# Order of the matmuls within an expert's weight block, and selections of results placed in groups of four

## The chip, the cores and the metric

The kernel runs on one core of one Trainium2 chip. The metric is the device time of one execution in microseconds (us). Engines are named as in the profile: PE is TensorE (PEld its weight loads), DVE is VectorE, ACT is ScalarE, POOL is GpSimd, SP is SyncE, whose queue issues the weight transfers.

## What is computed

Two layers over 256 context and 512 latent tokens of width 1024. Each has a mixer (a recurrent branch and a long convolution, merged by gates) and then a mixture of experts, which the change touches:

```python
def expert_block(args):
    xblk, e = args
    return (jax.nn.silu(xblk @ w_gate[e]) * (xblk @ w_up[e])) @ w_down[e]
yb = lax.map(expert_block, (xb, block_e)).reshape(n_blocks * MOE_BLOCK, d)
y_slots = jnp.zeros((n_slots, d), yb.dtype).at[order].set(yb[dest])
return (y_slots.reshape(n_tok, TOP_K, d) * wts[..., None].astype(yb.dtype)).sum(1)
```

There are 16 experts; each token goes to two of them. All three weights of an expert are 1024 x 1024 in float32. Layer 0 sends 768 tokens through the experts, layer 1 the 512 latent tokens alone.

## The kernel before

Experts are sorted by how many tokens they got, and each rank has a fixed number of rows (`CAPS`, line 25): in layer 0 96, 256, 192, three of 160, four of 96 and six of 64; in layer 1 96, 192, 128, five of 96 and eight of 64. `TURN` (line 26) sets which ranks run together: two experts in a pass alternate chunk by chunk, and two experts of 64 rows can share one unit of 128 rows (`n == 2`). The passes of layer 1 are 0; 15 with 14; 1 beside 13 with 12; 2 beside 3; 4 beside 5; 6 beside 7; 11 with 10; 9 with 8. Those of layer 0 are 0; 2 beside 11 with 10; 1 beside 13 with 12; 3 beside 6; 4 beside 7; 5 beside 8; 9; 15 with 14.

An expert's weights come as six chunks `c` (gate, gate, up, up, down, down; 512 columns each), a chunk as two halves `s2` of 1 MB, four weight rows `k` of 128 x 512 each, so eight rows `k` in a chunk. `weights` (line 2085) issues a half on SP's queue into one of `RAW` = 5 buffers in layer 0, 10 in layer 1; a transfer waits until the last reader of its buffer is done.

An expert's rows are cut into pieces (line 1915) of 128, 64 or 32. In layer 0 a piece of 128 is "split": weights and operand go into a high and a low part (`weight_parts`, on ACT and DVE) and three matmuls per `k` (`mm3`, lines 593 to 595). Unsplit pieces take plain float32 matmuls: with 64 rows two of them lie side by side in the array's columns, with 32 rows four (lines 1949 and 1952; a float32 matmul shows as two records). So 96 rows are pieces of 64 and 32, 160 rows a split 128 and a 32, 192 rows a 128 (split in layer 0) and a 64.

`chunk` (line 1929) sets the order of TensorE's work. Within a half it goes over quarters `s` of two rows `k`; in each quarter every piece takes its two rows (a 32-row piece takes all four rows of the half in the second quarter). A chunk of 96 rows is thus 64, 32, 64, 32; one of 192 rows 128, 64, four times over.

What follows a chunk is put off: `self.after` holds it, and `flush` (line 2097) runs it after the first half of the next chunk. For a gate chunk that is the SiLU on ACT (line 1972); for an up chunk a product on DVE (line 1977) and transposes on TensorE (line 1990), which give rows 0 to 3 of the down chunks' operand from the first up chunk, rows 4 to 7 from the second; for a down chunk the sum over the array's column groups (`total`, line 1997, ACT and DVE) and the weighting (line 2059).

In layer 1, and for the last pass of layer 0, the result of a unit is not stored but added to the tokens' rows by a selection matrix: `add` (line 2009) casts it into a high and a low part (`yh`, `yl`, one buffer each) and queues one closure per block of 128 tokens (4 in layer 1, 6 in layer 0). A block is two matmuls (lines 2030 and 2031) into one of two `pt` buffers, and one DVE addition of it into `xs` (line 2033). `some` (line 2102) places `SOME` = 1 queued block after each quarter, so up to four in a chunk. In the last pass of layer 0 (`early`, line 1761) POOL adds up the stored results beside the last two experts; line 2046 on DVE needs a product of POOL (line 1784).

The engines' programs follow this order of emission, except where the framework's planner, which orders by its own estimates of what is ready, moves an instruction ahead of one that it takes to be waiting.

Of the kernel before, what the change touches and what calls it, by code (L numbers as in the profile page):

```python
# [29 lines left out]
XLO = (1, 3), ()  # L30
EARLY_V = ()
HH = [slice(0, 512), slice(512, 1024)]
SOME, YB, YW = 1, 1, (3, 2)
XG, XB = (3, 4), (2, 3)
FIN = (2, 3, 4, 5, 0, 1), (2, 3, 4, 5)
GMR = 6, 6
# [543 lines left out]
class Kern:  # L580
# [1326 lines left out]
    def expert(self, l, P, evs, units, xs):  # L1907
# [8 lines left out]
        for u, (rows, *_) in enumerate(units):  # L1916
            split = self.splits(l, rows, n)
# [6 lines left out]
        mine = [[p for p in pieces if p[3] == j] for j in range(n)]  # L1924
        hilo = any(p[4] for p in pieces)
        bank = lambda: P["pg"].tile([128, 512], F32, name="acc", tag="acc", bufs=6)
        mm = nc.tensor.matmul

        def chunk(c, j, ops, after):
            acc = [bank() for p in mine[j]]  # L1930
            for s2 in range(2):
                raw = self.raws.pop(0) if self.raws else self.weights(l, P, evs[j], c, s2)
                for s in range(2):
                    if hilo:
                        hi, lo = self.weight_parts(P, raw, s)
                    for (u, w, o, _, split), a in zip(mine[j], acc):
                        op, G = ops[u], 128 // w
                        if split:
                            for i in range(2):
                                k = 4 * s2 + 2 * s + i  # L1940
                                self.mm3(a, op[:, k, 0], op[:, k, 1], hi[:, i], lo[:, i], k == 0, k == 7)
                            continue

                        for i in (range(2 * s, 2 * s + 2) if w > 32 else range(4 * s)):
                            k = 4 * s2 + i
                            x = op[:, k, o:o + w]
                            if c < 4:
                                for g in range(G):
                                    mm(a[w * g:w * g + w, 0:4 * w], x, raw[:, i, 4 * w * g:4 * w * g + 4 * w], start=k == 0, stop=k == 7)  # L1949
                            else:  # L1950
                                g = k % G
                                mm(a[w * g:w * g + w], x, raw[:, i], start=k < G, stop=k >= 8 - G)  # L1952
                    self.some()
                if s2 == 0:
                    self.flush()
            self.after = lambda: after(acc)

        act, ops, out, g, sel = {}, {}, {}, {}, {}
# [114 lines left out]
        for h in range(2):  # L2073
            for j in range(n):
                chunk(h, j, xs, gate(j))
            yield
            for j in range(n):
                chunk(2 + h, j, xs, up(h, j))
            yield
        for h in range(2):  # L2080
            for j in range(n):
                chunk(4 + h, j, ops, down(h, j))
            yield
# [82 lines left out]
```

## Time and profile before

| | |
|---|---|
| median of 3 runs | 3333.3 us (3323.03 to 3336.45) |
| the profiled execution | 3332.37 us |
| its span | 3330.5 us |
| TensorE busy | 3022.4 us (91%) |
| VectorE, ScalarE, GpSimd busy | 1715.7 us (52%), 1145.2 us (34%), 556.2 us (17%) |
| mean granted TensorE clock | 0.937 of full |
| weight transfers of the experts | 384 of 1 MB |

The experts of layer 0 run from about 1104 us to 1783 us of the span, those of layer 1 from about 2683 us to 3305 us; between and before them lie the mixers. A row of the timeline gives the start, the length, the engine, the source line, the operation, the tile written and the tiles read, and how many records were merged; in brackets stands the engine's idle time before it and what ended it.

### The profile page before, as it was taken

How to read it: one execution, taken by the hardware profiler on the slowest of the kernel's cores; microseconds unless marked ns; L12 is line 12 of the kernel's file. 1: busy time of each engine (PE TensorE's matmuls, PEld its weight loads, DVE VectorE, ACT ScalarE, POOL GpSimd, SP SyncE). 2: the span in 40 equal slices, each digit the busy share in tenths (PEclk: the TensorE clock that was granted, in tenths of full speed). 3: DMA queues.
4: the chain of work that ended last, by engine and by line, in shares of the span. 5: the costliest groups of instructions: out<-in, count | busy, mean ns of one | idle time of the engine just before them, and what ended most of it. 6: DMA issues, size and time to landing. Idle time of an engine off the chain costs nothing. (4 is left out here: it accounts for less than half of the span.)

```text
span 3330.5 us, 61793 instructions
## 1 busy us (share of the span) xinstructions
PE 3022.4 (91%) x25406; PEld 2022.0 (61%) x25406; DVE 1715.7 (52%) x3074; ACT 1145.2 (34%) x2309; POOL 556.2 (17%) x436
## 2 busy tenths in 40 slices
PE   7999998988897899999965999988988889999995
PEld 5778865766776556666632867657756644444443
DVE  4456526788758333344308447377776641223343
ACT  3443216555322233344313433365634211111111
POOL 1001203333014000000044001244410400000000
PEclk9999998899998899999986999977999889999998
DMA  5453272111362888988993473522124489888885
GB/s 221 132 155 93 89 275 89 48 54 38 129 233 104 308 333 332 359 315 315 324 351 132 135 218 113 182 71 62 48 70 138 182 330 391 285 289 305 281 339 244
DMA packets 215206, 675.42 MB, mean 203 GB/s; under 512 B 70949, under 2 KB 98886, under 8 KB 163464
## 3 DMA queue, kind: packets, MB, share of 16 engines
q1 hardware_dynamic: 186120, 588.36, 50.0%
q10 hardware_dynamic: 22512, 61.55, 5.3%
q0 software_dynamic: 6288, 21.50, 1.9%
q8 instruction: 203, 3.33, 0.4%
q14 instruction: 83, 0.68, 0.1%
HBM read 615.03 MB, written 56.30 MB: 202 GB/s over the span
## 5 line engine op out<-in xcount | busy, mean ns | idle before, releaser
L1949 PE MATMUL acc<-raw,x 128*64 128x256 f32 (+1 forms) x7168 | 590.0, 336 | 9.9 <-DMA raw<-in_w_exp 9.8
L1949 PEld LDWEIGHTS acc<-raw,x 128*64 128x64 f32 (+1 forms) x7168 | 349.8, 125 | 237.7 <-issue 124.9
L589 DVE TENSOR_TENSOR lo<-raw,hi 128x1024 fp32r<-128x1024 f32 x190 | 230.2, 1233 | 316.2 <-ACT hi L588 309.5
L1952 PE MATMUL acc<-raw,a 128*64 128x512 f32 (+2 forms) x1376 | 316.5, 607 | 1.1 <-SPq L1790 1.1
L588 ACT CAST hi<-raw 128x1024 fp32r<-128x1024 f32 x190 | 193.7, 1046 | 245.6 <-PE px L852 118.5
L1977 DVE TENSOR_TENSOR act<-acc,act 128x256 f32<-128x256 f32 (+2 forms) x98 | 41.6, 429 | 366.9 <-PE acc L1949 332.0
L848 PE MATMUL pl<-xh,hi 128*128 128x512 f32 x560 | 226.6, 405 | 0.1
L853 PE MATMUL pl<-xh,lo 128*128 128x512 f32 x560 | 223.7, 399 | 0.5 <-DVE lo L589 0.5
L849 PE MATMUL pl<-xl,hi 128*128 128x512 f32 x560 | 223.2, 399 | 0.0
L1116 PE MATMUL gp<-gx,raw 128*128 128x512 f32 (+1 forms) x352 | 179.7, 629 | 1.5 <-ACT gs L1118 1.4
L1952 PEld LDWEIGHTS acc<-raw,a 128*64 128x64 f32 (+2 forms) x1376 | 77.3, 130 | 169.2 <-issue 157.8
L1874 POOL DMA_INDIRECT xg<-hd,idx x31 | 31.2, 1005 | 775.3 <-PE pt L1892 696.1
L1995 ACT COPY a<-pt 128x256 f32<-128x256 f32 (+2 forms) x86 | 27.6, 350 | 331.4 <-PE pt L1990 331.4
L848 PEld LDWEIGHTS pl<-xh,hi 128*128 128x128 f32 x560 | 106.2, 190 | 37.4 <-issue 14.0
L2033 DVE TENSOR_TENSOR xs<-pt,xs 128x512 f32<-128x512 f32 x116 | 78.6, 690 | 89.2 <-PE pt L2031 88.7
L853 PEld LDWEIGHTS pl<-xh,lo 128*128 128x128 f32 x560 | 106.6, 190 | 18.0 <-issue 9.2
L849 PEld LDWEIGHTS pl<-xl,hi 128*128 128x128 f32 x560 | 106.3, 190 | 15.9 <-issue 8.2
L1972 ACT ACTIVATE act<-acc 128x256 f32<-128x256 f32 (+2 forms) x98 | 38.0, 389 | 218.8 <-PE acc L1949 187.1
L851 PE MATMUL px<-xh,hi 128*128 128x256 f32 x376 | 109.7, 292 | 0.0
L855 PE MATMUL px<-xh,lo 128*128 128x256 f32 x376 | 108.8, 290 | 0.0
L852 PE MATMUL px<-xl,hi 128*128 128x256 f32 x376 | 108.0, 287 | 0.4 <-DVE xl L589 0.2
L311 PE MATMUL pO<-T,K 128*128 128x192 f32 (+1 forms) x320 | 85.0, 378 | 25.6 <-DVE T L330 24.9
(611 smaller groups left out, 6220.6 us busy)
## 6 DMA issues: line engine op xcount, KB each, us to landing
raw<-in_w_exp SPq DMA_DIRECT2D x384, 1024.0 KB
mraw<-in_w_mod SPq DMA_DIRECT2D x64, 512.0 KB
raw<-in_w_in SPq DMA_DIRECT2D x36, 512.0 KB
rkk<-rkk SPq DMA_DIRECT2D x24, 768.0 KB
raw<-in_w_in ACTq DMA_DIRECT2D x34, 512.0 KB
mraw<-in_w_mod SPq DMA_DIRECT2D x12, 1024.0 KB
raw<-in_w_in SPq DMA_DIRECT2D x32, 256.0 KB
wb<-in_w_branch SPq DMA_DIRECT2D x32, 256.0 KB
```

Of the source, the lines that this page charges most:

```text
L311: nc.tensor.matmul(pO[:, jj, 0:192], lO, T[c][kO, j, 1, :], start=True, stop=True)
L588: self.nc.scalar.copy(hi, src)
L589: (engine or self.nc.vector).tensor_tensor(lo, src, f32(hi), ALU.subtract)
L848: mm(pl, hi[:, k], xh[:, k, L], start=f, stop=False)
L849: mm(pl, hi[:, k], xl[:, k, L], start=False, stop=False)
L851: mm(px, hi[:, k], xh[:, k, X], start=f, stop=False)
L852: mm(px, hi[:, k], xl[:, k, X], start=False, stop=False)
L853: mm(pl, lo[:, k], xh[:, k, L], start=False, stop=e)
L855: mm(px, lo[:, k], xh[:, k, X], start=False, stop=e)
L1116: nc.tensor.matmul(p[:, :n], raw[k // 4][:, k % 4], self.gx[:, k, a - T0:a - T0 + n], start=k == 0, stop=k == 7)
L1949: mm(a[w * g:w * g + w, 0:4 * w], x, raw[:, i, 4 * w * g:4 * w * g + 4 * w], start=k == 0, stop=k == 7)
L1952: mm(a[w * g:w * g + w], x, raw[:, i], start=k < G, stop=k >= 8 - G)
```

## The change

`chunk` collects both halves of a chunk. Split pieces keep their order. After them each unsplit piece takes all eight rows `k` in one run, piece after piece, instead of two (or four) at a time in turn with the others; in chunk 4 alone, whose second half needs operands that the flush makes, it takes four rows in each half. The flush keeps its place after the first half in chunk 4 and for experts with a split piece; else it comes after the first piece's run, or, where a chunk has one piece, at the end of the chunk. `some` is called once, at the end of a chunk, and places up to four blocks.

```diff
--- before.py
+++ after.py
@@ -30,7 +30,7 @@
 XLO = (1, 3), ()
 EARLY_V = ()
 HH = [slice(0, 512), slice(512, 1024)]
-SOME, YB, YW = 1, 1, (3, 2)
+SOME, YB, YW = 4, 1, (3, 2)
 XG, XB = (3, 4), (2, 3)
 FIN = (2, 3, 4, 5, 0, 1), (2, 3, 4, 5)
 GMR = 6, 6
@@ -1928,31 +1928,35 @@
 
         def chunk(c, j, ops, after):
             acc = [bank() for p in mine[j]]
+            raws = []
             for s2 in range(2):
-                raw = self.raws.pop(0) if self.raws else self.weights(l, P, evs[j], c, s2)
+                raws.append(self.raws.pop(0) if self.raws else self.weights(l, P, evs[j], c, s2))
                 for s in range(2):
                     if hilo:
-                        hi, lo = self.weight_parts(P, raw, s)
+                        hi, lo = self.weight_parts(P, raws[s2], s)
                     for (u, w, o, _, split), a in zip(mine[j], acc):
-                        op, G = ops[u], 128 // w
                         if split:
                             for i in range(2):
                                 k = 4 * s2 + 2 * s + i
-                                self.mm3(a, op[:, k, 0], op[:, k, 1], hi[:, i], lo[:, i], k == 0, k == 7)
-                            continue
-
-                        for i in (range(2 * s, 2 * s + 2) if w > 32 else range(4 * s)):
-                            k = 4 * s2 + i
-                            x = op[:, k, o:o + w]
-                            if c < 4:
-                                for g in range(G):
-                                    mm(a[w * g:w * g + w, 0:4 * w], x, raw[:, i, 4 * w * g:4 * w * g + 4 * w], start=k == 0, stop=k == 7)
-                            else:
-                                g = k % G
-                                mm(a[w * g:w * g + w], x, raw[:, i], start=k < G, stop=k >= 8 - G)
-                    self.some()
-                if s2 == 0:
+                                self.mm3(a, ops[u][:, k, 0], ops[u][:, k, 1], hi[:, i], lo[:, i], k == 0, k == 7)
+
+                for q, ((u, w, o, _, split), a) in enumerate(zip(mine[j], acc)):
+                    for k in range(4 * s2, 4 * s2 + 4) if c == 4 else range(8 * s2):
+                        if split:
+                            break
+                        x, raw, G = ops[u][:, k, o:o + w], raws[k // 4][:, k % 4], 128 // w
+                        if c < 4:
+                            for g in range(G):
+                                mm(a[w * g:w * g + w, 0:4 * w], x, raw[:, 4 * w * g:4 * w * g + 4 * w], start=k == 0, stop=k == 7)
+                        else:
+                            g = k % G
+                            mm(a[w * g:w * g + w], x, raw, start=k < G, stop=k >= 8 - G)
+                    if q == 0 and s2 == 1 and c != 4 and len(acc) > 1:
+                        self.flush()
+                if s2 == 0 and (c == 4 or hilo):
                     self.flush()
+            self.flush()
+            self.some()
             self.after = lambda: after(acc)
 
         act, ops, out, g, sel = {}, {}, {}, {}, {}
```

## Rows read from the trace of the kernel before

**Rows 1.** Busy time by stretch: us, PE, PEld, DVE, ACT, POOL, PEclk, DMA share, GB/s
```profile
1391.00:1475.00 84.00, 84.00 (x910) 52.43 (x910) 39.30 (x45) 37.81 (x56) 2.72 (x3) 1.00 0.90 327
...
3012.50:3102.50 90.00, 90.00 (x959) 43.04 (x958) 31.92 (x57) 16.19 (x36) 0.00 (x0) 1.00 0.80 281
...
3192.50:3242.50 50.00, 48.75 (x336) 25.40 (x334) 14.79 (x27) 7.12 (x15) 0.00 (x0) 1.00 0.99 397
```

**Rows 2.** Waits of SP's transfer queue, layer 0: us in total, times, longest
```profile
SPq L2089 <- PE acc L1949: 312.5, 110, 19.2
...
SPq L2089 <- DMA raw<-in_w_exp: 8.2, 9, 1.3
```

**Rows 3.** Groups of PE instructions, 2690 to 3300 us: busy, mean ns, idle before
```profile
L1949 PE MATMUL acc<-raw,x 128*64 128x256 f32 (+2 forms) x3488 | 330.9, 347 | 0.0
...
L2030 PE MATMUL pt<-yh,sel 96*128 96x512 f32 (+2 forms) x100 | 49.2, 501 | 5.2 <-ACT yh L588 4.9 <-DVE xs L2033 0.3
...
L1990 PE MATMUL pt<-con,act 128*128 128x128 f32 x88 | 16.5, 292 | 3.0 <-DVE act L1977 3.0
```

**Rows 4.** Timeline of PEld within a pass of two 96-row experts, layer 1
```profile
3027.50 1.49 PEld L1949 LDWEIGHTS acc<-raw,x 128*64 128x64 f32 x16 [0.20 <-issue]
3029.37 0.81 PEld L1949 LDWEIGHTS acc<-raw,x 128*32 128x32 f32 x32 [0.39 <-issue]
3030.39 1.49 PEld L1949 LDWEIGHTS acc<-raw,x 128*64 128x64 f32 x16 [0.20 <-issue]
```

**Rows 5.** Timeline of PE: two rows of a 64-row piece, then eight together
```profile
1170.20 1.08 PE L1949 MATMUL acc<-raw,x 128*64 128x256 f32 x8
1171.21 0.50 PE L593 MATMUL acc<-hi,x 128*128 128x512 f32 x1
...
3206.33 3.67 PE L1949 MATMUL acc<-raw,x 128*64 128x256 f32 x32
3209.94 0.44 PE L1990 MATMUL pt<-con,act 128*128 128x128 f32 x2
```

**Rows 6.** Timeline of PE: the same point of two successive chunk turns, layer 0
```profile
1391.00 1.08 PE L1949 MATMUL acc<-raw,x 128*32 128x128 f32 x32
...
1404.72 1.08 PE L1949 MATMUL acc<-raw,x 128*32 128x128 f32 x32
```

**Rows 7.** Timeline of PE: one selection block between runs of weight rows
```profile
3011.78 0.50 PE L2030 MATMUL pt<-yh,sel 128*128 128x512 f32 x1
3012.11 0.40 PE L2031 MATMUL pt<-yl,sel 128*128 128x512 f32 x1
3012.44 2.10 PE L1949 MATMUL acc<-raw,x 128*64 128x256 f32 x40
```

**Rows 8.** Timeline of PE: two blocks back to back, and what follows them
```profile
3237.92 0.50 PE L2030 MATMUL pt<-yh,sel 128*128 128x512 f32 x1
...
3239.05 3.65 PE L1952 MATMUL acc<-raw,a 128*64 128x512 f32 x16
```

**Rows 9.** All selection blocks: counts, and ns min/median/max of DVE's addition
```profile
L2030 PE MATMUL pt<-yh,sel x104: 389/498/797, 2723.4 to 3303.4; 96*128 96x512 f32 x48, 128*128 128x512 f32 x48, 64*128 64x512 f32 x8
...
L2033 DVE TENSOR_TENSOR xs<-pt,xs x116: 675/691/694, 1761.8 to 3304.6; 128x512 f32<-128x512 f32 x116
```

**Rows 10.** Timeline of ACT and DVE: from a down chunk's sum to its low part
```profile
3009.21 0.59 ACT L2001 ACTIVATE sum<-acc 64x512 f32<-64x512 f32 x1 [3.42 <-PE acc L1952]
...
3016.03 0.68 DVE L589 TENSOR_TENSOR yl<-y,yh 96x512 fp32r<-96x512 f32 x1
```

**Rows 11.** Timeline of PE: first and last record of the last four blocks
```profile
3300.70 0.73 PE L2030 MATMUL pt<-yh,sel 128*128 128x512 f32 x2 [2.91 <-ACT yh L588]
...
3303.90 0.63 PE L2031 MATMUL pt<-yl,sel 128*128 128x512 f32 x1
```

**Rows 12.** Timeline, last pass of layer 0: a wait for weights, the longest wait, POOL's end
```profile
1708.77 1.95 PE L1949 MATMUL acc<-raw,x 128*64 128x256 f32 x16 [1.91 <-DMA raw<-in_w_exp]
...
1738.72 0.69 PE L1990 MATMUL pt<-con,act 128*128 128x128 f32 x2 [16.79 <-DVE act L1977]
...
1765.56 2.37 POOL L1782 TENSOR_TENSOR xs<-x,xs 128x1024 f32<-128x1024 f32 x1
```

## The prediction, made before the changed kernel ran

> **What bounds the kernel now.** I first read the busy time of each engine in stretches of the two expert stages, to see who is full where the change acts. In the passes of layer 0 around 1400 us and in those of layer 1 around 3050 us TensorE is busy for the whole stretch, VectorE for under half of it, at full granted clock [rows 1]. Only where two experts of 64 rows run alone do the transfers come level, at 397 GB/s and a DMA share of 0.99. Next the waits of the queue that issues the weights: in layer 0 it waits 312.5 us for matmuls that still hold a buffer and 8.2 us for the transfers themselves [rows 2]; TensorE holds up the weights, not the reverse. Then TensorE's own groups in layer 1: no idle time before 3488 records of the hidden chunks, and 5.2 us in all before the selections [rows 3]. So a microsecond of TensorE saved here is a microsecond of the kernel, until a transfer or a chain on VectorE comes level.
>
> TensorE is full, but not of columns. A change of piece costs time. Four weight rows of a 64-row piece take 1.87 us from start to the next piece's start, four of a 32-row piece 1.02 [rows 4]. Two rows of a 64-row piece alone take 1.01, eight in one run 3.61 [rows 5]. From two to eight is 2.60 for six rows, 0.433 each, so a run has a fixed cost of 1.01 - 0.87 = 0.14 us; from four to eight it comes out as 2 x 1.87 - 3.61 = 0.13. I take 0.14 a run.
>
> **Part one, the runs of eight.** A chunk of 96 rows goes from four runs to two, in five chunks of six (chunk 4 keeps four). One of 192 rows goes from eight to two, and from eight to four in chunk 4. One of 160 goes from four to two in five chunks. Experts of 64, 128 and 256 rows have one kind of piece and gain nothing.
> Layer 1: six experts of 96 give 6 x 5 x 2 = 60 runs, the one of 192 gives 5 x 6 + 4 = 34; 94 x 0.14 = 13.2 us.
> Layer 0: the three passes of 160 beside 96 give 3 x 5 x 4 = 60; one turn of both chunks takes 13.72 us now [rows 6] and should take 13.16. The first 96 gives 10 more: 70 x 0.14 = 9.8 us. The 192 (34 runs) and the ninth expert (10) I cost at nothing: with five buffers their weights are nearly the bound, and the first half's buffer is now held to the last piece's fourth row instead of to mid-chunk.
> Part one: 23.0 us. Bounds: an eight-row run of a 32-row piece is not in the trace. If all its gain is absent, half is left, 11.5. At most each run saves the 0.20 us by which the weight loads pause before a 64-row run [rows 4], for all 208 runs: 42 us.
> The Trainium skill, "TensorEngine Tiling (Array Packing)", Key Properties, says that changing the tiling mode, not just the tile, drains TensorE; "TensorE: Matmul & The Clock Gate", Single matmul latency, gives a constant of 398 cycles at 2.4 GHz that a lone matmul can't hide, 0.166 us. By that, as an estimate, 164 runs would give 27 us; the rows' 0.14 decides.
>
> **Part two, selections in fours.** There are 104 blocks in layer 1 [rows 9]; the last four come after all matmuls in either kernel, so 25 groups of four are moved. (The 12 of layer 0 run in its tail, behind POOL.) One block between runs takes 0.66 us to the next run's start [rows 7], and cuts a run, 0.14: four cost 3.2. Two back to back take 1.13 [rows 8], so the second adds 0.47. The third needs the buffer of the first, whose addition takes 0.69 on VectorE [rows 9]: it can start at 0.66 + 0.69 = 1.35 and the fourth at 2.04, so the group ends at 2.51, with its cut 2.65. Gain 0.55 a group, 13.8 us. If the planner fills the pauses with matmuls, the third and fourth stand alone: 1.13 + 0.14 + 2 x 0.80 = 2.87, still a gain.
> Against it: a group waits at its head for the cast of its result, with all of TensorE's later work behind it. From the sum's first step to the end of the low part it takes 3016.03 + 0.68 - 3009.21 = 7.5 us, additions of earlier blocks among them [rows 10]. In a pass of 96-row experts a group comes one chunk (about 5.5 to 5.8 us) after its sum can start, or a chunk and a group (8.1) once groups follow one another. So the first group of a pass waits, for between nothing and 1.7 us; five passes have such a chain, at 1.3 that is 6.5. Of the 5.2 us idle before selections now, I let 3 go, since those of the 64-row pairs now come after a whole chunk. Part two: 13.8 - 6.5 + 3 = 10.3 us. Bounds: with no waits and additions hidden, a group is 0.66 + 3 x 0.47 + 0.14 = 2.2, gain 25; the other end is the last group, below.
>
> **Edits at no cost.** The flush after the first piece: the product on VectorE for the transposes runs under that piece's 3.61 us, as now under the half chunk's 2.9; uncovered, it shows as the 3.0 us now seen before line 1990 [rows 3]. The flush at a chunk's end for 64-row pairs: same number of transposes, and the product is done earlier. No transfer and no instruction is added or dropped; SP's queue keeps its order.
>
> Sum: 23.0 + 10.3 = 33.3 us against the profiled execution's 3332.4, which lies 0.9 below the median of the runs: 3299 us, by the terms' bounds 3272 to 3316.
>
> **Rivals.**
> *The sums set the pace.* In a 96-row pass a chunk's chain of 7.5 us plus a fourth addition of 0.69 is 8.2, level with TensorE's 5.5 + 2.65 = 8.1. If it comes out at the 9.0 that a chunk with four blocks takes now (5.78 + 3.2), part two's 13.8 and part of the runs in some 20 chunks (20 x 0.28 = 5.6) are lost: 3299 + 18 = 3317. For it: VectorE and ScalarE take turns in that chain. Against: the planner starts the next sum early. The Trainium skill's tiling page, PSUM Bottleneck, speaks for it: tiling speeds up TensorE but not the emptying of PSUM.
> *The order doesn't come out.* The planner cuts runs where it takes the second half for not landed, and scatters the groups. For it: blocks that the code emits one at a time already stand in pairs [rows 8]. Against: in the passes of 96 rows the runs are as emitted. Next to nothing is gained: 3330.
> *Layer 0 starves.* Five buffers, held longer, leave TensorE waiting as it does in the last pass, 1.91 us at a time [rows 12]; once in each of the 12 chunks of the 192 and of the ninth expert that is 23: 3299 + 23 = 3322. Against: the pairs need 4 MB in 13 us, and the layer's queue waits for TensorE [rows 2].
> *The head of each group waits (slower).* The last group waits 2.91 us for its cast [rows 11]. If each of the 25 did, 73 us stand against 13.8 and part one's 23.0: 3332 + 36 = 3368. It turns slower where the wait passes (13.8 + 23.0)/25 = 1.5 us a group. For it: TensorE's order is fixed, nothing overtakes. Against: the last group has no chunk before it to hide its chain; the others have 3.6 to 8.1 us.
> *The stall in layer 0's tail goes.* TensorE waits 16.79 us for a product queued on VectorE behind one that needs POOL [rows 12]. If the new order puts it first, up to 13 us more are gained, since the stage ends near 1783 us and POOL's last sum at 1767.9 in any case: 3286.
>
> **How the numbers follow.** Forecast 0.55, sums set the pace 0.13, order not out 0.10, starving 0.06, waiting heads 0.10, tail stall gone 0.06. The runs shown differ by 0.4%, so 0.5%, 17 us, is about what can be told from no change: under 3316 counts as faster (0.55 + 0.06), 3316 to 3350 as the same (0.13 + 0.10 + 0.06), above as slower (0.10). The range runs from the sum with its better bounds, 3272, to the order that doesn't come out, 3330; outside lie the waiting heads and the ends of the sum, under 0.2.
>
> **What would show it.** Right: 64-row runs of eight at 3.6 us and 32-row runs of eight near 1.9 in the timeline, a turn of 160 and 96 rows near 13.2 us, one of two 96-row experts near 10.9 without blocks; four blocks together in about 2.5; idle time before line 2030 under 12 us. Wrong: 32-row runs of eight at 2.0 (the fixed cost isn't there), runs still of four, idle time of tens of us before line 2030, or waits for the experts' weights before line 1949 in layer 0 above the few that stand there now.

## The result and the profile after

The changed kernel takes 3292.45 us (median of 4 runs, 3289.95 to 3302.53) against 3330.77 for the kernel before (4 runs, 3323.03 to 3336.45): a ratio of 0.9876, 95% interval 0.9854 to 0.9898, so 1.2% faster. The forecast was 3299. The profiled execution took 3294.88 us, its span is 3293.0.

The page's first lines show as many records of TensorE as before (25406), in 46 us less of its time and with a span 37.5 us shorter:

```profile
span 3293.0 us, 61763 instructions
...
PE 2976.3 (90%) x25406; PEld 2036.7 (62%) x25406; DVE 1711.4 (52%) x3074; ACT 1143.1 (35%) x2309; POOL 556.0 (17%) x436
```

The busy time by stretch, in the columns of [rows 1], for the passes of 160 beside 96 rows in layer 0 and for the pairs of 96 rows in layer 1:

```profile
1391.00:1475.00 84.00, 83.99 (x919) 55.41 (x918) 40.61 (x46) 38.41 (x57) 2.72 (x3) 1.00 0.88 328
2990.00:3080.00 90.00, 90.00 (x1038) 48.65 (x1038) 34.86 (x63) 17.09 (x39) 0.00 (x0) 1.00 0.79 295
```

In both stretches TensorE is still busy all the time at the full granted clock (1.00). In 90 us of layer 1 it now starts 1038 records where it started 959 in [rows 1]. The gain is thus shorter work in a full engine, not a wait removed. The groups of TensorE's instructions in layer 1, 2668 to 3270 us, say the same of the idle time (line 1950 was 1949, 2034 was 2030, 1994 was 1990):

```profile
L1950 PE MATMUL acc<-raw,x 128*64 128x256 f32 (+2 forms) x3584 | 327.6, 345 | 1.0 <-issue 1.0
...
L2034 PE MATMUL pt<-yh,sel 96*128 96x512 f32 (+2 forms) x104 | 47.6, 468 | 8.4 <-ACT yh L588 7.8 <-DVE xs L2037 0.7
...
L1994 PE MATMUL pt<-con,act 128*128 128x128 f32 x88 | 16.5, 291 | 3.0 <-DVE act L1981 3.0
```

Here the heads of the groups wait 7.8 us for their casts. The window of [rows 3] ends before the last group; over the whole of layer 1 the waits of the kernel before have the same 7.8 us in the same 5 waits. What the products (line 1981) hold up is also unchanged at 3.0.

**The runs.** TensorE's weight loads within a pass of two 96-row experts show the order that was asked for:

```profile
3000.70 3.22 PEld L1950 LDWEIGHTS acc<-raw,x 128*64 128x64 f32 x32 [0.20 <-issue]
3004.30 1.69 PEld L1950 LDWEIGHTS acc<-raw,x 128*32 128x32 f32 x64 [0.38 <-issue]
3006.19 3.22 PEld L1950 LDWEIGHTS acc<-raw,x 128*64 128x64 f32 x32 [0.20 <-issue]
```

Eight rows of a 64-row piece take 3.60 us from start to start, eight of a 32-row piece 1.89. A chunk is 5.49 us; in [rows 4] it is twice 1.87 + 1.02, so 5.78.

**The groups.** They don't come out whole. First TensorE, then VectorE, beside a group of four:

```profile
2983.38 0.50 PE L2034 MATMUL pt<-yh,sel 128*128 128x512 f32 x1
2983.71 0.40 PE L2035 MATMUL pt<-yl,sel 128*128 128x512 f32 x1
2983.95 0.40 PE L2034 MATMUL pt<-yh,sel 128*128 128x512 f32 x1
2984.18 0.40 PE L2035 MATMUL pt<-yl,sel 128*128 128x512 f32 x1
2984.51 0.65 PE L1950 MATMUL acc<-raw,x 128*64 128x256 f32 x2
2985.08 0.50 PE L2034 MATMUL pt<-yh,sel 128*128 128x512 f32 x1
...
2985.74 0.65 PE L1950 MATMUL acc<-raw,x 128*64 128x256 f32 x4
2986.33 0.50 PE L2034 MATMUL pt<-yh,sel 128*128 128x512 f32 x1
...
2986.99 5.12 PE L1950 MATMUL acc<-raw,x 128*64 128x256 f32 x90
```

```profile
2984.15 1.29 DVE L2037 TENSOR_TENSOR xs<-pt,xs 128x512 f32<-128x512 f32 x2 [0.43 <-PE pt L2035]
2985.47 0.69 DVE L2008 TENSOR_TENSOR sum<-acc,sum 64x512 f32<-64x512 f32 x1
2986.19 0.69 DVE L2037 TENSOR_TENSOR xs<-pt,xs 128x512 f32<-128x512 f32 x1
2987.10 0.69 DVE L2037 TENSOR_TENSOR xs<-pt,xs 128x512 f32<-128x512 f32 x1 [0.22 <-PE pt L2035]
```

Two blocks run back to back, then the two result buffers are full until VectorE has added them. The planner fills the gap with 2 and then 4 records of the next run. No idle time appears here, so no view of waits shows this: the price is two more changes of tile. From 2983.38 to 2986.99 are 3.61 us; six records at 0.108 (0.433 us for the four of a weight row) were work that had to be done anyway, so the group costs 2.96 us. The same reckoning over the 25 groups of layer 1 ahead of the last gives 72.6 us, 2.90 on the mean and from 2.4 to 3.6; none is whole, nine are in three parts.

**Layer 0.** The transfers of the experts, by the waits of SP's queue and of TensorE from 1104 to 1783 us:

```profile
SPq L2093 <- PE acc L1950: 312.8, 116, 14.6
...
SPq L2093 <- DMA raw<-in_w_exp: 9.4, 9, 1.3
```

```profile
PE pt L1994 <- DVE act L1981: 15.3, 6, 12.3
PE acc L1950 <- DMA raw<-in_w_exp: 12.4, 9, 1.9
...
PE acc L593 <- ACT hi L588: 5.2, 4, 1.8
PE acc L1953 <- DMA raw<-in_w_exp: 1.9, 2, 1.7
```

The queue still waits for TensorE, as in [rows 2]. The long wait in the tail, 16.79 us in [rows 12], is 12.3. Waits for weights and for their high parts grew by 6.4 us in all (12.4 + 5.2 + 1.9 now, 9.8 + 3.3 before, where the down chunks show no wait for weights).

**A finer measure than the whole.** What lies outside the experts' passes moves by several us from one profile to the next, though the experiments leave it alone: the first pass starts at 1103.0 us in the kernel before, at 1109.1 in the changed one, at 1096.0 in a kernel below. So I also compare the **expert stages**: from the first operand transpose (line 1892) of layer 0's first pass to that of its last pass, plus from layer 1's first to the end of the span. Each is read from one profile. Where kernels of this document give TensorE the same matmuls in the same order, layer 0's part agrees within 2.7 us (561.3, 559.3 and 558.6 in the changed kernel and two below) and layer 1's within 1.0 (624.9, 624.6 and 624.5; 649.2 and 650.3).

| kernel | layer 0 | layer 1 | expert stages |
|---|---|---|---|
| before | 1103.0 to 1677.0: 574.0 | 2681.3 to 3330.5: 649.2 | 1223.2 |
| after | 1109.1 to 1670.4: 561.3 | 2668.1 to 3293.0: 624.9 | 1186.2 |

The stages give 37.0 us, 12.7 in layer 0 and 24.3 in layer 1. The spans differ by 37.5, so what lies outside (the first mixer 6.1 us longer, layer 0's last pass and the second mixer 6.6 shorter) nearly cancels.

### The profile page after: what moved, and what is told of

Same layout as the page of the kernel before. It is cut to its first block, busy times and chain, and to the rows that moved or that the text cites. A ratio compares the mean times of both kernels' runs of the same rounds, so it can differ in the third digit from the quotient of the medians.

```text
span 3293.0 us, 61763 instructions
## 1 busy us (share of the span) xinstructions
PE 2976.3 (90%) x25406; PEld 2036.7 (62%) x25406; DVE 1711.4 (52%) x3074; ACT 1143.1 (35%) x2309; POOL 556.0 (17%) x436
## 3 DMA queue, kind: packets, MB, share of 16 engines
q1 hardware_dynamic: 186120, 588.36, 49.4%
## 5 line engine op out<-in xcount | busy, mean ns | idle before, releaser
L1950 PE MATMUL acc<-raw,x 128*32 128x128 f32 (+1 forms) x7168 | 569.5, 333 | 13.5 <-DMA raw<-in_w_exp 12.4
L1950 PEld LDWEIGHTS acc<-raw,x 128*32 128x32 f32 (+1 forms) x7168 | 362.3, 125 | 207.5 <-issue 86.4
L1953 PE MATMUL acc<-raw,a 128*64 128x512 f32 (+2 forms) x1376 | 300.3, 604 | 2.0 <-DMA raw<-in_w_exp 1.9
```

What stands on the lines that cost most here:

```text
L1950: mm(a[w * g:w * g + w, 0:4 * w], x, raw[:, 4 * w * g:4 * w * g + 4 * w], start=k == 0, stop=k == 7)
L1953: mm(a[w * g:w * g + w], x, raw, start=k < G, stop=k >= 8 - G)
```

## The experiments

### Groups alone, runs alone

Before's order with four blocks once a chunk:

```diff
-SOME, YB, YW = 1, 1, (3, 2)
+SOME, YB, YW = 4, 1, (3, 2)
...
-                    self.some()
                 if s2 == 0:
                     self.flush()
+            self.some()
```

> Part two alone: the matmuls stand in the order of before, and up to four blocks are placed at the end of a chunk. Theory (the two parts add up: runs some 23 us, groups some 10): about 3320 us, runs of four weight rows (64 rows at 1.87 us, 32 rows at 1.02), and one turn of 160 and 96 rows at 13.7 us as before. Rival 1 (the groups carry most of the 38 us): about 3300. Rival 2 (the groups gain nothing, it is all the runs): 3331. Rival 3 (heads of groups wait): above 3331, with more than the 7.8 us of waiting for yh in layer 1.

The changed order with single blocks, one after each four rows of a piece:

```diff
-SOME, YB, YW = 4, 1, (3, 2)
+SOME, YB, YW = 1, 1, (3, 2)
...
                             mm(a[w * g:w * g + w], x, raw, start=k < G, stop=k >= 8 - G)
+                        if k % 4 == 3:
+                            self.some()
...
-            self.some()
```

> Part one alone: runs of eight as in the change, but the blocks are placed one by one, one after each four weight rows of a piece (half of them cut a run in its middle, half stand between two pieces). Theory: the runs' 23 us are there, the groups' 10 to 15 are missing: 3305 to 3310 us, and the turn of 160 and 96 rows is near 13.2 us. Rival (single blocks between pieces cost no more than blocks in groups): as the changed kernel, 3292. Rival (the runs alone gain nothing): 3331.

Groups alone: 3326.64 us, ratio 0.9972 (0.9956 to 0.9988); the expert stages are 1212.9, a gain of 10.3. Runs alone: 3298.27 us, ratio 0.9884 (0.9861 to 0.9907); stages 1190.8, a gain of 32.4. Together they gain 37.0, so the runs are worth 26.7 to 32.4, the groups 4.6 to 10.3, according to which is there first. Both parts are real and the runs are the larger one. Layer 0's stage has no blocks, so the groups are better read from layer 1 alone: 9.9 us with the old order, 6.6 with the new. The runs alone did better than the 3305 to 3310 that was expected.

The changes of tile shape can be counted in TensorE's records. With groups alone the stages have 199 more of them than the changed kernel's, 104 in layer 0 and 95 in layer 1; 26.7 us for 199 are 0.134 each.

### The price of a change of piece

The runs of eight are cut into runs of two rows, the pieces in turn (chunk 4 keeps its runs of four):

```diff
+                rows = range(4 * s2, 4 * s2 + 4) if c == 4 else range(8 * s2)
+                step = 4 if c == 4 else 2
+                for at in rows[::step]:
+                    for (u, w, o, _, split), a in zip(mine[j], acc):
+                        for k in range(at, at + step):
...
+                    if at == 2 and s2 == 1 and c != 4 and len(acc) > 1:
                         self.flush()
```

> The cost of a change of piece, multiplied: as the changed kernel, but unsplit pieces take two weight rows in turn, so that a chunk of 96 rows has eight runs (two in the changed kernel, four before) in five chunks of six, and the 192 of layer 1 eight as well. Groups of four and all else as in the changed kernel. Theory (each run costs 0.14 us whatever its length): eleven experts of 96 rows and the one of 192 in layer 1 get 6 x 5 x 12 = 360 runs more, 50 us: 3342 against 3292, a chunk of two 96-row pieces at 6.3 us against 5.49. Rival (what helped is not the number of changes but when the second piece's weights are read, or the flush): near the kernel before or the changed one, under 15 us more.

It took 3363.79 us, ratio 1.0101 (1.0068 to 1.0135), slower than the kernel before; the stages are 1255.1, 68.9 above the changed kernel, more than expected. The weight loads show a run of two of each piece in a gate or up chunk, then two 32-row runs in down chunks: one of four rows in chunk 4 (8 records) and one of two rows in chunk 5 (4 records):

```profile
3080.55 0.38 PEld L1953 LDWEIGHTS acc<-raw,x 128*32 128x32 f32 x16 [0.39 <-issue]
3081.12 0.63 PEld L1953 LDWEIGHTS acc<-raw,x 128*64 128x64 f32 x8 [0.20 <-issue]
3082.14 0.38 PEld L1953 LDWEIGHTS acc<-raw,x 128*32 128x32 f32 x16 [0.39 <-issue]
...
3084.58 0.16 PEld L1956 LDWEIGHTS acc<-raw,a 128*32 128x32 f32 x8 [0.81 <-issue]
3085.57 0.31 PEld L1997 LDWEIGHTS pt<-con,act 128*128 128x128 f32 x3 [0.84 <-issue]
...
3104.62 0.14 PEld L1956 LDWEIGHTS acc<-raw,a 128*32 128x32 f32 x4 [0.81 <-issue]
3105.60 0.20 PEld L1956 LDWEIGHTS acc<-raw,a 128*64 128x64 f32 x4 [0.84 <-issue]
```

A pair of runs takes 1.59 us, a chunk of four pairs 6.36. That is 0.87 above 5.49 for six more runs, 0.145 each, and 360 runs were added (the trace has 361 more changes of tile shape): 50 to 52 us. The rest is in the last chunk. There a 32-row piece uses a different column group for each row, so a run of two fills two of the four and still takes 0.98 us, as the run of four does that fills all of them (0.99). Four runs of two are 3.92, where a run of eight with three changes would be 1.89 + 0.44 = 2.33; 1.6 us in each of 11 chunks (six experts of 96 rows in layer 1, five in layer 0) are 17.5. Together 68 to 70, as measured. The expectation had left out that last part.

### The 192 of layer 0, costed at nothing

That expert alone keeps two rows in each quarter, as before:

```diff
+                        elif hilo and w == 64:
+                            for k in range(4 * s2 + 2 * s, 4 * s2 + 2 * s + 2):
+                                rows(a, u, w, o, raws[s2], k)
...
-                        if split:
+                        if split or hilo and w == 64:
```

> The changed kernel, but the expert of 192 rows in layer 0 keeps the order of before (its 64-row piece takes two rows after each quarter of the split piece). Theory (its 34 saved runs are eaten by weights that come late, since the first half's buffer is held longer): the passes of the 192 and of the next expert are as long or up to 5 us shorter, and TensorE's waits for a cast and for weights in that pass go: 3287 to 3294. Rival (the runs pay there too): 3 to 6 us longer, 3296 to 3298.

It took 3296.0 us, ratio 0.9886 (0.9845 to 0.9927), and its stages are 1186.2, the same as the changed kernel's. The interval of the runs is too wide to tell the theory from the rival, so I look at the stretch from the operand transposes of the 192 to those of the first 160. It takes 224.0 us here, 223.0 in the changed kernel, and 221.3 and 221.7 in the kernels with runs alone and with pairs (below), whose matmuls there are the changed kernel's. Here 20 changes of tile shape come back (78 for 58), 2.8 us at 0.14, and 2.1 us of TensorE's idle time go (7.6, now 5.5). So the runs of this expert seem to save work, and waits to take most of it back; within 3 us the sum is nothing.

### What hides the flush

The flush goes ahead of the first piece's run in the chunks in which the change put it behind:

```diff
+                if s2 == 1 and c != 4:
+                    self.flush()
...
-                    if q == 0 and s2 == 1 and c != 4 and len(acc) > 1:
-                        self.flush()
```

> The changed kernel with the flush ahead of the first piece's run instead of after it (chunk 4 and experts with a split piece as they were): the transposes of an up chunk's products stand right behind that chunk's last matmul. Theory (the prediction's cover: the first piece's 3.6 us hide the product on VectorE): some 50 flushes lie open at about 0.6 us each, the wait that the kernel before shows in five places: 25 to 35 us more than the changed kernel, nearly all as idle time before line 1994. Rival (the planner moves matmuls ahead of the waiting transposes): under 8 us.

It took 3306.21 us, ratio 0.9918 (0.9889 to 0.9946); the stages are 1198.0, 11.8 more than in the changed kernel, 8.0 of them in layer 1. That is neither the 25 to 35 us of the theory nor the rival's under 8. The waits for the product grew only from 3.0 to 3.9 us in layer 1. The timeline of TensorE shows the rest, the cut kernel first, then a flush in the changed one:

```profile
3096.66 0.44 PE L1994 MATMUL pt<-con,act 128*128 128x128 f32 x2
3097.02 0.65 PE L1952 MATMUL acc<-raw,x 128*64 128x256 f32 x2
3097.60 0.33 PE L1994 MATMUL pt<-con,act 128*128 128x128 f32 x1
3097.86 5.55 PE L1952 MATMUL acc<-raw,x 128*64 128x256 f32 x94
```

```profile
3093.89 0.55 PE L1994 MATMUL pt<-con,act 128*128 128x128 f32 x3
3094.37 1.84 PE L1950 MATMUL acc<-raw,x 128*32 128x128 f32 x60
```

Three transposes take 0.48 us at a change of piece that is there anyway. Ahead of the first piece they take 1.20, of which 0.22 is the two records moved between them: 0.50 us more. The 200 transposes stand in 62 stretches in the changed kernel and in 78 here; 16 x 0.50 is 8 us, and with the 0.9 of waiting 9 of the 11.8 are found; the rest is no more than the scatter of layer 0. Again most of the loss is cuts and not idle time.

### Two blocks at the end of each piece, and a third result buffer

Pairs after each piece's run, in place of four at the chunk's end:

```diff
-SOME, YB, YW = 4, 1, (3, 2)
+SOME, YB, YW = 2, 1, (3, 2)
...
+                    if s2 == 1:
+                        self.some()
                     if q == 0 and s2 == 1 and c != 4 and len(acc) > 1:
                         self.flush()
...
-            self.some()
```

> The changed kernel with two blocks after each piece's run instead of four after the chunk, and placed ahead of the flush that may queue new ones: a pair never needs a third buffer, and stands where the piece changes anyway, so it cuts no run. Theory (a group of four is cut by matmuls in its middle while its third block waits for a buffer; in the pass of 6 and 7 a block costs about 0.86 us all in): a block falls to about 0.57 us, half of 1.13, for some 100 blocks 15 to 25 us less than the changed kernel, 3268 to 3278. Rival (VectorE's additions and sums set the pace in the down chunks): no change, 3288 to 3296. Rival (the planner moves the blocks anyway): no change.

The changed kernel with one result buffer more, and one accumulation bank less (the same edit at all five places):

```diff
-        bank = lambda: P["pg"].tile([128, 512], F32, name="acc", tag="acc", bufs=6)
+        bank = lambda: P["pg"].tile([128, 512], F32, name="acc", tag="acc", bufs=5)
...
-                p = P["pg"].tile([128, 512], F32, name="pt", tag="pt")
+                p = P["pg"].tile([128, 512], F32, name="pt", tag="pt", bufs=3)
```

> The changed kernel with three buffers for blocks and transposes instead of two, and five banks for accumulation instead of six. Theory (the second half of a group waits for a buffer): three blocks stand together, a group loses one of its two cuts, 0.2 to 0.4 us of 25 groups, 5 to 10 us less than the changed kernel: 3282 to 3288. Rival (the buffers are not what holds a group): the same within 3 us. Rival (five accumulation banks hold up the next chunk): slower than the changed kernel, with waits of TensorE on ACT or DVE before the experts' matmuls.

Both edits together:

> Two blocks after each piece's run, ahead of the flush, and three buffers for blocks and transposes with five accumulation banks: the two edits that were tried alone, together. Theory (both remove the same thing, the cuts and waits within a group, and the third buffer serves the transposes of the next pass's operands besides): about as the third buffer alone, 3268 to 3276 on the scale on which the kernel before takes 3334. Rival (they add up): 3250 to 3258.

Pairs: 3279.99 us, ratio 0.9836 (0.9812 to 0.986), stages 1168.8. Third buffer: 3272.24, ratio 0.9807 (0.9784 to 0.9831), stages 1163.6, 22.6 less than the changed kernel and well above the expected gain. Both: 3268.26, ratio 0.9797 (0.9754 to 0.9839), stages 1163.7. They don't add up, so for the most part they remove the same thing. A pair in the kernel with pairs, then a whole group with three buffers and VectorE beside it:

```profile
2968.20 0.50 PE L2035 MATMUL pt<-yh,sel 128*128 128x512 f32 x1
...
2969.34 1.95 PE L1950 MATMUL acc<-raw,x 128*32 128x128 f32 x64
```

```profile
2962.12 0.50 PE L2034 MATMUL pt<-yh,sel 128*128 128x512 f32 x1
...
2964.30 5.56 PE L1950 MATMUL acc<-raw,x 128*64 128x256 f32 x96
```

```profile
2962.88 2.48 DVE L2037 TENSOR_TENSOR xs<-pt,xs 128x512 f32<-128x512 f32 x4 [0.42 <-PE pt L2035]
```

A pair takes 1.14 us, two of them 2.28, and sits at a change of piece that exists anyway. The group shown with three buffers is uncut and takes 2.18; 12 of the 25 are whole like it, and all 25 take 61.8 us, where the changed kernel's take 72.6. That is 10.8 us less.

The stages have to be read by layer here. In layer 1 pairs gain 14.7 us, where 25 x (2.90 - 2.28) would be 15.5; the third buffer gains 14.9, both together 18.0. So the groups are 10.8 of the third buffer's 14.9. In layer 0, whose stage has no blocks, the third buffer shows 7.6 us, and 3.0 of these are the measure's: the operand transposes of the last pass start 18 records earlier in the work, and the stage ends with them. To the first expert matmul of the last pass, which has the same 5040 records in all these kernels, layer 0 takes 567.7 us in the changed kernel, 563.1 with the third buffer, 566.2 with both edits. So the third buffer's 22.6 us are 19.6, and what it gives in layer 0 is hardly more than the scatter there.

### Is the third buffer's gain its own? Is a fourth worth more?

The same buffer edit in the kernel before:

> The order of before and single blocks, with three result buffers for selections and transposes in place of two, and five accumulation banks in place of six. The question is whether the 22 us that the third buffer gave in the changed kernel are its own or belong to the groups of four. Theory (most of it belongs to the groups: only back-to-back blocks need the third buffer, and before places them one or two at a time; what is left is the 16 operand transposes of each pass and the pairs): 5 to 12 us faster than before, about 3322. Rival (the buffer is worth as much in any order): 20 us or more, about 3311. Rival (five banks hold up the chunks in the old order): no faster than before.

The changed kernel with four result buffers and four accumulation banks:

> The changed kernel with four result buffers and four accumulation banks. Theory (with three buffers the group of four already runs uncut, so a fourth has nothing left to remove, and four banks are enough for two chunks of two pieces): within 5 us of the kernel with three, 3268 to 3277. Rival (the fourth buffer lets the last block start earlier too): 3262 or less. Rival (four banks are too few: a chunk waits for its accumulators to be summed, above all where a pass has pieces of three kinds): 3290 or more, with idle time before the experts' first matmuls of a chunk.

In the kernel before it gives 3326.68 us, ratio 0.9982 (0.9968 to 0.9997), and 10.8 us in the stages (1212.4), 3.0 of them the measure's again: 7.8. In layer 1 it is 4.1, against 14.9 in the changed kernel. The difference, 10.8, is what was found in the groups themselves.

With four: 3258.95 us, ratio 0.9782 (0.9754 to 0.9811). The stages are 1158.3, 5.3 below those with three: 8.2 less in layer 1, 2.9 more in layer 0. The theory was wrong in its ground: with three buffers 13 of the 25 groups were still cut. Now 21 are whole, and the 25 take 54.9 us, 6.9 less than with three. The group shown takes 2.04 us:

```profile
2947.70 0.50 PE L2034 MATMUL pt<-yh,sel 128*128 128x512 f32 x1
...
2949.74 5.56 PE L1950 MATMUL acc<-raw,x 128*64 128x256 f32 x96
```

The intervals of the three fastest kernels (three buffers, pairs with three, four) overlap, so which is best among them stays open; all three are faster than both kernels of this case. Of the 18.9 us by which the span with four is shorter than with three (3246.0 against 3264.9), 13.6 lie outside the expert stages, so most of the 13 us between their medians can't be put down to the fourth buffer.

### How near the weights are: four buffers in layer 0

In the changed kernel, and then in the kernel before:

```diff
-RAW = 5, 10
+RAW = 4, 10
```

> The changed kernel with four weight buffers in layer 0 in place of five. In the new order a chunk's first half is held until the last unsplit piece has passed its fourth row. Theory (the held half is what five buffers cover, so that with four the new order starves more than the old one): 25 to 45 us slower than the changed kernel, and its loss at least 10 us above that of the old order with four. Rival (the two orders lose the same, the holding costs nothing): both 5 to 20 us. Rival (a fifth buffer is not needed at all): within 5 us of the kernel with five.

> The kernel before with four weight buffers in layer 0 in place of five. Theory (the old order frees the first half at mid-chunk, so it needs fewer buffers): 5 to 20 us slower than before, at least 10 us less than the new order loses. Rival (the two orders lose the same): as much as the new one, within 5 us.

The new order takes 3342.86 us, ratio 1.0032 (1.0011 to 1.0053), the old one 3354.53, ratio 1.007 (1.0038 to 1.0102). Against five buffers the new order loses 50.4 us in the medians and 49.4 in the stages (1235.6), the old one about 25 (stages 1247.9, 24.7 more). The new order thus loses another 25 us once a buffer is missing. The three passes of 160 beside 96 rows show it: 258.1 us become 285.0 in the new order, 264.9 become 270.1 in the old one. Both losses are a little above what was expected. One such pass, with five and with four buffers in the new order:

```profile
1458.80:1543.30 84.50, 84.30 (x925) 55.78 (x921) 41.12 (x47) 39.54 (x58) 2.72 (x3) 1.00 0.88 324
```

```profile
1486.00:1579.40 93.40, 89.05 (x925) 55.81 (x921) 41.12 (x48) 39.10 (x58) 2.72 (x3) 1.00 0.81 294
```

About half of the 8.9 us is idle time; the other half is longer work with the same 925 records at the same clock. The idle time is waiting for the weights' high and low parts (2.2 and 2.0 us). The transfers are no common floor for both orders: their share fell from 0.88 to 0.81, and the new order is slower here than the old one. That it is the holding of the first half fits all this, but no run changes the holding alone. In the timeline of the second kernel the run of the 32-row piece is torn up, since the planner puts parts of it where it takes the split rows for late:

```profile
1504.53 0.86 PE L1950 MATMUL acc<-raw,x 128*32 128x128 f32 x22
...
1508.35 1.07 PE L1950 MATMUL acc<-raw,x 128*32 128x128 f32 x28
...
1510.92 0.43 PE L1950 MATMUL acc<-raw,x 128*32 128x128 f32 x8
```

## Why the prediction was right

**Bound.** It started from TensorE being full of work, not of waits. After the change it still is, and but for the kernels with four weight buffers the gains and losses above are nearly all time within its rows.

**Part one, the runs: right, a little small.** 23.0 us was predicted, 26.7 is measured with the groups there. The fixed cost of a run, 0.14 by [rows 4, 5], held for both pieces: 32-row runs of four and of eight give 2 x 1.02 - 1.89 = 0.15, the runs of two 0.145. The rule of the Trainium skill, "TensorEngine Tiling (Array Packing)", Key Properties, that a change of the tiling mode drains TensorE, agrees with these rows in kind: the price is there at each change of piece, 0.14 us. By layer, both parts together: layer 1 24.3 for 13.2 + 10.3, layer 0 12.7 for 9.8. Within layer 0 the passes of 160 beside 96 rows gave 6.8 (264.9 to 258.1) for 8.4, the first 96 nothing for 1.4, the ninth expert 1.5 where nothing was predicted, and the stretch with the 192 and the 256 gave 4.4 (227.4 to 223.0), again for nothing. That stretch has 30 changes of tile shape fewer (88, now 58), 4.2 us at 0.14, but also 1.7 us more idle time, so some 2 us of it stay open, about what layer 0 scatters.

**The 192 and starving.** To cost its 34 runs at nothing was right within 3 us, as it seems because saved work and new waits nearly cancel. The rival in which layer 0 starves was wrong with five buffers: 6.4 us more of waiting, not 23. The danger is real, and one buffer away: with four, the new order loses twice what the old one does.

**Part two, the groups: the sum right, by terms that were off and cancelled.** 10.3 predicted; in layer 1, where they run, 9.9 with the old order and 6.6 with the new. The group's price was taken as 2.65 for an uncut group. It came out near the alternative that the text gave at 2.87, with the third and fourth block alone: 2.90 on the mean. That takes 6.3 us off the 13.8. The 6.5 us for waiting heads did not come: the waits for the casts are 7.8 us in both kernels. Nor did the 3 us of old waits go. So the terms as they came out give 13.8 - 6.3 = 7.5, between the two measured values; that the forecast's 10.3 lies as near to them as it does is luck.

**The flush: right at no cost, wrong in the sign by which a cost would show.** I wrote that uncovered it would show as idle time. Ahead of its cover it costs 11.8 us, and almost none of it is idle: the planner moves matmuls into the gap and the cut is paid for.

**The rivals.** *The sums set the pace*: no, line 1950 waits 1.0 us in all of layer 1. What VectorE does set is the pace within a group, through the two buffers. The Trainium skill, "Perfetto Trace Analysis", Matmuls, asks that independent matmul groups rotate through different PSUM banks, so that the emptying of one overlaps the next. The runs with more buffers agree: a group takes 2.90 us on the mean with two, 2.47 with three, 2.20 with four. *The order doesn't come out*: the runs did, with few cuts; none of the 25 groups did as a whole. *The head of each group waits*: no. *The tail's stall goes*: no, it shrank by 4.5 us.

**The bounds.** The forecast's 3299 follows from its terms; its bounds, 3272 and 3316, don't. With the 42 and the 25 of the better bounds the sum is 3265, and the groups' lower bound is not worked out. In the rival of the sums 13.8 + 5.6 is 19.4, not 18. Nothing in the verdict hangs on either.

## What to carry to other kernels

On a full engine, count the changes of tile shape: here each cost 0.13 to 0.15 us, and some two hundred fewer were most of the gain. Where a planner may fill gaps, a wait that you take away or add can appear as cuts in its neighbours' runs, so compare the start-to-start time of the same work in two timelines, not the idle columns. And before work is gathered into bursts, count the buffers that a burst needs: the third result buffer gave about 20 us, 10.8 of them in the groups of four.

## What was not expected of the hardware

In a down chunk of the kernel with runs of two, a 32-row run takes 0.98 us with two weight rows and 0.99 with four (1.0 in 39 and in 28 places): with two of the four column groups in use the time doesn't fall. A 64-row run there takes 1.0 us with one row as with two. And four additions of 128 x 512 from PSUM that follow one another on VectorE take 2.48 us, 0.62 each, where one alone takes 0.69.
